# Holding the next weights' split behind the copies of the value blocks, and the output's last 512 columns as two products and two sums of 256

## The chip, the cores and the metric

One core of a Trainium2 chip runs the whole program in one launch. The metric is the time of one execution in microseconds, as the device reports it. The kernel before has three such runs and one more that was profiled.

## The reference

Two layers of an encoder trunk for 256 tokens of 1024 channels in float32. Cut to what matters here:

```
h = rms_norm(x, norm1_g[l])
aq, ak, av, bq, bk, bv, cq, ck, cv, dq, dk, dv, g = split_parts(h @ w_in[l])
o_a = diff_attention(rope(norm(aq)), rope(norm(ak)), av, ...)      # 4 heads
o_b = gqa_attention(axial_rope(norm(bq)), axial_rope(norm(bk)), bv)
o_c = dilated_attention(rope(norm(cq)), rope(norm(ck)), cv)        # 3 groups of 512 columns
o_d = neighbourhood_attention(norm(dq), norm(dk), dv, rpb[l])
merged = sum_i sigmoid(g_i) * (o_i @ w_branch[l, i])
x = x + merged @ w_out[l]
x = x + (silu(a) * b) @ w_down[l]      # a, b: convolved halves of rms_norm(x) @ w_up[l]
```

The columns of `w_in` that make `dv`, `av` and the three groups of `cv` are the "value blocks": five per layer.

## The kernel before, in words

Every weight matrix passes through as a row of jobs of 1 MB. A job's `load` (L277) is one transfer on SyncE's queue into one of three `w` buffers, issued three jobs ahead. A job's weights are cut into two halves, and `split` turns each half into a float32r pair: ScalarE casts it to `hi` (L288), VectorE subtracts to get `lo` (L292). There are five `hi` and five `lo` buffers. TensorE multiplies each half in three products per step, `hi` by the rounded activations, `lo` by them, and `hi` by the activations' rest (L345, L346, L347 in `mm3`). One half feeds twelve matmuls of 512 columns.

`run` walks through the jobs in order. For job j it issues the load, splits half 2j+3, calls what the table `sched` has for the place (j, -1), then four quarters of the job's matmuls with a second split behind the second quarter and the calls of `sched` behind each. The attention units, the copies and the transposes are all such calls. The accumulators of the weight products are four PSUM banks ("mm"), score and transpose tiles have three ("ts"), and one bank ("o") holds the attention's outputs and now and then a transpose. `ORDER` gives the sequence of blocks: qD kB kD qB kA vD qA vA gD0 kC1 kC0 qC1 ... vC0 ... vC1 vC2 and so on.

A value block (`vblock`) takes two jobs. Behind the last quarter of the second, `ev` copies its two accumulators into a `t4` buffer: for vD, vA and vC0 by two ScalarE copies of 512 columns (L838), for vC1 and vC2 by ScalarE and VectorE in halves (L844). For vD, sixteen small transfers on SyncE's queue then gather shifted windows of these values (`windows`, L854).

`behind` holds what is issued inside it to a place behind the named instructions. `self.hold` is a dictionary of such instructions by place, which `run` asks at two of its splits. The sequence of instructions on each engine is settled when the program is built, by a scheduler that lets a ready instruction pass one that is not ready. On the chip each engine then runs its list as written.

An attention unit of mixers A or B runs: two scores on TensorE (L545), maximum on VectorE (L626), two exponentials on ScalarE (L630), reciprocal on VectorE (L642), for B two scalings on ScalarE (L645), four transposes on TensorE (L549), a copy on ScalarE (L656), products with the values into "o" (L545), and a rounding of the result on ScalarE (L449) and VectorE (L455). For D the exponentials stand in L611.

At the end of the last layer `down` accumulates 256 x 1024 outputs in four banks, and `fin` adds each to the residual (L1194) and stores it by two transfers (L1197), one on SyncE's and one on ScalarE's queue.

Of the kernel before, what the change touches and what calls it, by code (L numbers as in the profile page):

```python
# [13 lines left out]
ALU = mybir.AluOpType  # L14
# [4 lines left out]
DEPTH = 2  # L19
# [70 lines left out]
class Trunk:  # L90
# [214 lines left out]
    def run(self):  # L305
        for j, job in enumerate(self.jobs):
            first, second = j in self.pairs, j - 1 in self.pairs
            self.load(j + LOAD_AHEAD)
            if not second and j > 1:
                self.split(2 * j + 3)  # L310
            for fn in self.sched.get((j, -1), []):
                fn()
            for q in range(4):

                src, sq = job, q
                if first:
                    src, sq = self.jobs[j + q // 2], q % 2
                elif second:
                    src, sq = self.jobs[j - 1 + q // 2], 2 + q % 2
                src["mm"](src["hl"], sq)  # L320
                if q == 1 and j not in self.late and j > 1:
                    with self.behind(self.hold.get((j, 0))):
                        self.split(2 * j + (3 if second else 4))
                for fn in self.sched.get((j, q), []):
                    fn()
            if second:
                with self.behind(self.hold.get((j, 1))):
                    self.split(2 * j + 4)
# [418 lines left out]
    def layer(self, l):  # L747
        nc = self.nc
        base = len(self.jobs)
        J = lambda s: base + s  # L750
# [30 lines left out]
        stt = [{"qT": {}, "kT": {}, "v": []} for _ in range(4)]  # L781
# [42 lines left out]
        def vblock(m, col0, g=0):  # L824
            cell = self.in_block(l, col0)
            slot[0] += 2
            e = slot[0] - 1

            def ev():
                v = stt[m]["v"]  # L830
                if g == 0:
                    v.append(self.t4([128, 2, 512]))
                elif g == 1:
                    v.extend([self.t4([128, 2, 512]), self.t4([128, 2, 512])])
                for t in range(2):
                    o = cell["o"][t]
                    if g == 0:
                        nc.scalar.copy(v[0][:, t, :], o)  # L838
                        continue

                    for b in range(2):
                        r = slice(64 * b, 64 * b + 64)
                        w = r if g == 1 else slice(64 - 64 * b, 128 - 64 * b)
                        (nc.scalar.copy if b == 0 else nc.vector.tensor_copy)(v[1 + t][w, b, :], o[r])  # L844

            def windows():

                v = stt[MD]["v"]
                for i in range(2):
                    v.append(self.t4([128, 2, 512]))  # L850
                for cb in range(4):
                    c0 = min(max(16 * cb - 8, 0), 32)
                    for u in range(4):
                        nc.sync.dma_start(v[1 + cb // 2][32 * u:32 * u + 32, cb % 2, :],  # L854
                                          v[0][64 * (u % 2) + c0:64 * (u % 2) + c0 + 32, u // 2, :])

            self.at(J(e), 3, ev)
            if m == MD:
                self.at(J(e + 1), 1, windows)
# [100 lines left out]
        for what in ORDER.split():  # L960
            kind, i, c = what[0], "ABCD".index(what[1]), int(what[2:] or 0)
            if what == "kB":
                bkv()
            elif kind in "qk":
                k = int(kind == "k")
# [198 lines left out]
        dacc = []  # L1164

        def down(i):
            def mm(hl, q):
                if not dacc:
                    dacc.extend([self.ps("ts"), self.ps("ts"), self.ps("ts"), self.ps("o")])
                steps = [(k, t) for k in range(2) for t in range(2)]  # L1170
                pairs = [(steps[q][0], steps[q][1], c) for c in range(2)]
                if i == 9:
                    pairs = [(q % 2, q // 2, c) for c in range(2)]
                if i == 10:
                    pairs = [(k, q // 2, q % 2) for k in range(2)]
                for k, t, c in pairs:
                    kt = 2 * i + k
                    g, gl = gh[kt // 4]
                    sl = slice(t * 128, (t + 1) * 128)
                    cs = slice(c * 512, (c + 1) * 512)  # L1180
                    self.mm3(dacc[2 * t + c][:, :], g[:, kt % 4, sl], gl[:, kt % 4, sl], hl[k][0][:, cs], hl[k][1][:, cs], kt == 0, kt == 21)

            self.add_jobs({"src": self.wsrc("w_down", l * DFF * DM, DM, i * 256, 2, 0, 1024), "mm": mm})
            slot[0] += 1
# [3 lines left out]
        e = slot[0] - 1  # L1188
        sst2 = {}

        def fin(t, c):
            cs = slice(c * 512, (c + 1) * 512)
            xs = self.x[:, t, cs]
            nc.vector.tensor_tensor(xs, xs, dacc[2 * t + c], ALU.add)  # L1194
            if l + 1 == DEPTH:
                for u in (2 * t, 2 * t + 1):
                    (nc.sync, nc.scalar)[u % 2].dma_start(self.rows("out", u, c * 512, 512), self.x[64 * (u % 2):64 * (u % 2) + 64, t, cs])  # L1197
                return
            if c == 0:
                sst2[t] = self.small("ss", 4)  # L1200
            self.sumsq(t, cs, sst2[t], c)
            if c == 1:
                xn = self.norm_vec(t, self.g1, sst2[t], 2)
                if t == 0:
                    self.hold[J(e), 0] = self.norm_tr(0, xn)
                else:
                    self.at(J(e + 1), 0, lambda: self.norm_tr(1, xn))
# [6 lines left out]
        for t in range(2):  # L1214
            for c in range(2):
                self.at(J(e - 1 + t), 2 + c, lambda t=t, c=c: fin(t, c))
# [129 lines left out]
```

## Time and profile before

| what | before |
|---|---|
| median of 3 runs | 1216.28 us (1216.18 to 1216.49) |
| the profiled execution's own time | 1213.31 us |
| its span | 1211.5 us |
| TensorE busy | 1195.5 us, 99% |
| VectorE busy | 907.7 us, 75% |
| ScalarE busy | 746.8 us, 62% |
| GpSimd busy | 180.1 us, 15% |
| moved by DMA | 212.01 MB, mean 175 GB/s |

The span is what the profile's records cover; the profiled execution's time also holds what lies around them, 1.8 us here. Busy shares are means over the whole span and say which engine leaves hardly any room: one at 99% is idle for 16 us in all, those of the beginning and the end among them.

### The profile page before, as it was taken

What the parts mean: (1) busy time and instruction counts of PE and PEld (TensorE: products, weight loads), DVE (VectorE), ACT (ScalarE), POOL (GpSimd) and SP (SyncE); (2) the same over time, 40 slices, a digit from 0 to 9 for tenths busy, and PEclk for the clock granted to TensorE, in tenths of its full rate; (3) what the DMA queues carried; (4) which work ended last, traced back from release to release, by engine and by line L of the source; (5) the groups of instructions that cost most, each with busy time, mean ns of one, the idle gap of its engine ahead of it and who ended that gap; (6) DMA issues with size and microseconds to landing.
All of it is one profiled execution on the core that took longest, in us unless ns stands there. A gap on an engine that the chain in (4) does not pass through costs nothing.

```text
span 1211.5 us, 17591 instructions
## 1 busy us (share of the span) xinstructions
PE 1195.5 (99%) x6656; PEld 992.9 (82%) x6656; DVE 907.7 (75%) x1491; ACT 746.8 (62%) x1311; POOL 180.1 (15%) x132
## 2 busy tenths in 40 slices
PE   8999999999999999999999999999999999999998
PEld 6887878887888888888878877788888888888886
DVE  6998777986565699988478868688855557889863
ACT  4557756556655476776355677655666545777751
POOL 0332130220000002121023211212200000121200
PEclk9999999999999999999999999999999999999999
DMA  8758355454554465566544754464544553655551
GB/s 281 229 168 242 105 174 170 143 191 174 160 187 143 138 203 172 171 203 208 209 161 156 216 198 140 151 197 144 187 142 140 174 174 105 209 191 171 194 213 66
DMA packets 127651, 212.01 MB, mean 175 GB/s; under 512 B 9069, under 2 KB 56781, under 8 KB 127566
## 3 DMA queue, kind: packets, MB, share of 16 engines
q1 hardware_dynamic: 125964, 206.16, 50.9%
q0 software_dynamic: 1280, 4.20, 1.6%
q8 instruction: 52, 0.85, 0.3%
q10 hardware_dynamic: 322, 0.53, 0.1%
q14 instruction: 33, 0.27, 0.1%
HBM read 203.53 MB, written 1.05 MB: 169 GB/s over the span
## 4 chain that ended last, share of the span: by engine, by line
PE 92%; DVE 4%; ACT 2%; issue 1%; POOL 0%; ACTq 0%; POOLq 0%; DVEq 0%
PE mm L345 18%; PE mm L346 18%; PE mm L347 18%; PE ts L1114 6%; PE mm L1114 5%; PE ts L545 4%; PE ts L1117 3%; PE mm L1117 3%; PE ts L347 2%; PE ts L346 2%; PE ts L345 2%; PE o L545 2%; PE ts L549 2%; DVE lo L292 2%; PE ts L515 1%; PE o L347 1%
## 5 line engine op out<-in xcount | busy, mean ns | idle before, releaser
L292 DVE TENSOR_TENSOR lo<-w,hi 128x1024 fp32r<-128x1024 f32 x376 | 457.4, 1225 | 176.2 <-ACT hi L288 172.6
L288 ACT CAST hi<-w 128x1024 fp32r<-128x1024 f32 x376 | 392.1, 1051 | 210.0 <-PE mm L347 155.9
L345 PE MATMUL mm<-hi,hT 128*128 128x512 f32 (+1 forms) x796 | 310.5, 392 | 2.4 <-DVE t L844 1.0
L346 PE MATMUL mm<-lo,hT 128*128 128x512 f32 (+1 forms) x796 | 308.2, 387 | 0.4 <-DVE lo L292 0.4
L347 PE MATMUL mm<-hi,hT 128*128 128x512 f32 (+1 forms) x796 | 307.5, 388 | 0.0
L345 PEld LDWEIGHTS mm<-hi,hT 128*128 128x128 f32 x796 | 149.7, 188 | 35.6 <-issue 2.9
L346 PEld LDWEIGHTS mm<-lo,hT 128*128 128x128 f32 x796 | 149.7, 188 | 30.3 <-issue 1.7
L347 PEld LDWEIGHTS mm<-hi,hT 128*128 128x128 f32 x796 | 149.5, 188 | 30.2 <-DVE hT L455 0.9
L1114 PE MATMUL mm<-hT,hi 128*128 128x512 f32 x352 | 124.4, 395 | 0.0
L1114 PE MATMUL ts<-hT,hi 128*128 128x512 f32 x320 | 114.2, 397 | 1.5 <-DVE e L1133 1.5
L1117 PE MATMUL mm<-hT,lo 128*128 128x256 f32 x352 | 94.7, 280 | 0.0
L1148 POOL TENSOR_TENSOR pt<-pt,e 128x256 f32<-128x256 f32 x44 | 58.1, 1339 | 223.3 <-DVE e L1144 203.4
L1117 PE MATMUL ts<-hT,lo 128*128 128x256 f32 x320 | 86.2, 280 | 0.0
L1114 PEld LDWEIGHTS mm<-hT,hi 128*128 128x128 f32 x352 | 65.8, 188 | 13.8 <-issue 0.2
L164 POOL TENSOR_TENSOR sm_qr<-sm_qr,mhalf 128x16 f32<-128x16 f32 (+1 forms) x24 | 74.7, 3111 | 2.0
L345 PE MATMUL mm<-hi,t 128*128 128x512 f32 (+1 forms) x192 | 73.5, 384 | 0.0
L346 PE MATMUL mm<-lo,t 128*128 128x512 f32 (+1 forms) x192 | 73.4, 382 | 0.0
L347 PE MATMUL mm<-hi,t 128*128 128x512 f32 (+1 forms) x192 | 72.9, 380 | 0.0
L1114 PEld LDWEIGHTS ts<-hT,hi 128*128 128x128 f32 x320 | 59.9, 188 | 15.5 <-DVE e L1133 3.1
L1117 PEld LDWEIGHTS mm<-hT,lo 128*128 128x128 f32 x352 | 66.2, 188 | 2.1 <-issue 0.2
L163 POOL TENSOR_SCALAR sm_qr<-sm_qr 128x16 f32<-128x16 f32 (+1 forms) x24 | 24.6, 1026 | 271.7 <-DVE sm_qr L504 271.6
L1117 PEld LDWEIGHTS ts<-hT,lo 128*128 128x128 f32 x320 | 60.1, 188 | 2.0 <-issue 0.2
(175 smaller groups left out, 1773.2 us busy)
## 6 DMA issues: line engine op xcount, KB each, us to landing
w<-in_w_in_dram SPq DMA_DIRECT2D x97, 1024.0 KB, 5.0
w<-in_w_up_dram SPq DMA_DIRECT2D x44, 1024.0 KB, 4.9
w<-in_w_down_dram SPq DMA_DIRECT2D x22, 1024.0 KB, 4.9
w<-in_w_branch_dram SPq DMA_DIRECT2D x16, 1024.0 KB, 5.0
w<-in_w_out_dram SPq DMA_DIRECT2D x8, 1024.0 KB, 4.9
t<-t POOLq DMA_DIRECT2D x16, 256.0 KB, 6.4
t<-t SPq DMA_DIRECT2D x32, 64.0 KB, 2.6
t<-in_rpb_dram SPq DMA_DIRECT2D x32, 62.5 KB, 5.5
```

What stands on the lines that cost most here:

```text
L163: nc.gpsimd.tensor_scalar(dst, ss, EPS, None, op0=ALU.add)
L164: nc.gpsimd.tensor_tensor(dst, dst, mh, ALU.pow)
L288: self.nc.scalar.copy(hi, w)
L292: self.last_split = self.nc.vector.tensor_tensor(lo, w, hi[:].bitcast(F32), ALU.subtract).ins
L345: mm(out, xh, wh, start=first, stop=False)
L346: mm(out, xh, wl, start=False, stop=False)
L347: self.last_mm = mm(out, xl, wh, start=False, stop=last).ins
L545: self.chain = (self.nc.tensor.matmul(out, stationary, moving, **kw).ins,)
L549: self.chain = (self.nc.tensor.transpose(out, src, self.ident).ins,)
L1114: wide = lambda: mm(o.rearrange("p (a s) -> p a s", a=2), h, self.hT[:, :, k, :], start=k == 0, stop=k == 7)
L1117: mm(o[:, :256], lo, self.hTh[:, k, :], start=False, stop=False)
L1148: nc.gpsimd.tensor_tensor(s[:, 256:], s[:, :256], y[:, 256:], ALU.mult)
```

## The change

Three edits. `ev` puts the last two of a value block's copies into `self.hold` for the job behind the block. `run` now asks this at the first split of each job, so that this split (its cast on ScalarE and its subtraction on VectorE) is issued behind these copies. And in the last layer the last quarter of the last job makes its 512 columns as two groups of 256, and `fin` adds and stores the last 512 columns in two steps of 256.

```diff
@@ run
             if not second and j > 1:
-                self.split(2 * j + 3)
+                with self.behind(self.hold.get((j, -1))):
+                    self.split(2 * j + 3)
@@ vblock, ev
-                v = stt[m]["v"]
+                v, copies = stt[m]["v"], []
...
                     if g == 0:
-                        nc.scalar.copy(v[0][:, t, :], o)
+                        copies = [nc.scalar.copy(v[0][:, t, :], o).ins]
                         continue
...
-                        (nc.scalar.copy if b == 0 else nc.vector.tensor_copy)(v[1 + t][w, b, :], o[r])
+                        copies.append((nc.scalar.copy if b == 0 else nc.vector.tensor_copy)(v[1 + t][w, b, :], o[r]).ins)
+
+                self.hold[J(e + 1), -1] = copies[-2:]
@@ down
+                if l + 1 == DEPTH and i == 10 and q == 3:
+
+                    pairs = [(k, 1, c) for c in (2, 3) for k in range(2)]
...
-                    cs = slice(c * 512, (c + 1) * 512)
-                    self.mm3(dacc[2 * t + c][:, :], g[:, kt % 4, sl], gl[:, kt % 4, sl], hl[k][0][:, cs], hl[k][1][:, cs], kt == 0, kt == 21)
+                    cs, out = slice(c * 512, (c + 1) * 512), dacc[2 * t + min(c, 1)]
+                    if len(pairs) == 4:
+                        cs, out = slice(c * 256, (c + 1) * 256), out[:, (c - 2) * 256:(c - 1) * 256]
+                    self.mm3(out, g[:, kt % 4, sl], gl[:, kt % 4, sl], hl[k][0][:, cs], hl[k][1][:, cs], kt == 0, kt == 21 and not (len(pairs) == 4 and c == 2))
@@ fin
+            if l + 1 == DEPTH:
+                n = 256 if (t, c) == (1, 1) else 512
+                for o in range(0, 512, n):
+                    cs = slice(c * 512 + o, c * 512 + o + n)
+                    xs = self.x[:, t, cs]
+                    nc.vector.tensor_tensor(xs, xs, dacc[2 * t + c][:, o:o + n], ALU.add)
+                    for u in (2 * t, 2 * t + 1):
+                        (nc.sync, nc.scalar)[u % 2].dma_start(self.rows("out", u, cs.start, n), self.x[64 * (u % 2):64 * (u % 2) + 64, t, cs])
+                return
             nc.vector.tensor_tensor(xs, xs, dacc[2 * t + c], ALU.add)
-            if l + 1 == DEPTH:
-                for u in (2 * t, 2 * t + 1):
-                    (nc.sync, nc.scalar)[u % 2].dma_start(self.rows("out", u, c * 512, 512), self.x[64 * (u % 2):64 * (u % 2) + 64, t, cs])
-                return
```

Line numbers behind the first edit are one higher in the change (L345 becomes L346, L838 becomes L839, L854 becomes L857). Because the scheduler builds a new sequence around the held splits, instructions move on every engine, nearly all of them around the value blocks; the number of each kind stays, but for the end's. Three places follow, all of the first layer; the second layer has the same three.

ScalarE around vA: `mm_1139` and `mm_1140` are vA's accumulators, `t_242_1310` the buffer they are copied to, `hi_1315` the half that the edit holds, `o_1281` an output of mixer D and `e_1218` the softmax of a unit of B. Before, two pieces of the list:

```order
L288 CAST hi_1237<-w_1133 128x1024 [waits DMAHW6_49,PE_49]
L288 CAST hi_1315<-w_1133 128x1024 [waits PE_49]
L656 COPY pt_1005<-ts_1004 128x512 [waits PE_49]
...
L656 COPY pt_1275<-ts_1274 128x512 [waits PE_49]
L449 CAST t_240_1298<-o_1281 128x16x16 x2
L838 COPY t_242_1310<-mm_1139 128x512
L838 COPY t_242_1310<-mm_1140 128x512
L288 CAST hi_1635<-w_1520 128x1024 [waits PE_49]
```

And in the change:

```order
L646 ACTIVATE e_1218<-e_1218,sm_cf_1227 128x256 [waits DVE_49]
L646 ACTIVATE e_1218<-e_1218,sm_cf_1227 128x256 [waits Activation_49]
L657 COPY pt_1268<-ts_1267 128x512 [waits PE_49]
L657 COPY pt_1275<-ts_1274 128x512 [waits PE_49]
L450 CAST t_240_1298<-o_1281 128x16x16 x2
L839 COPY t_242_1310<-mm_1139 128x512 [waits DMAHW7_49,DMAHW0_49]
L839 COPY t_242_1310<-mm_1140 128x512
L288 CAST hi_1315<-w_1133 128x1024
L288 CAST hi_1333<-w_1197 128x1024 [waits DMAHW7_49]
L288 CAST hi_1379<-w_1197 128x1024
```

The copies stand behind the same neighbours in both lists, those of `o_1281`; the cast of `hi_1315` and the casts that follow it (`hi_1333`, `hi_1379`, `hi_1395`, `hi_1458`, and five more that stood ahead of the copies before) have moved back behind them.

TensorE at the same place: `ts_1161` and `ts_1351` are scores of B, `ts_1209` the transposes of the softmax `e_1162` that comes out of `ts_1161`. Before:

```order
L346 MATMUL mm_1319<-lo_1316,hT 128x512
L545 MATMUL ts_1161<-t_78_466,t_126_725 128x256 [waits DVE_49,PE_49]
L545 MATMUL ts_1161<-t_78_466,t_126_725 128x256 x3
L347 MATMUL mm_1319<-hi_1315,hT 128x512
L345 MATMUL mm_1320<-hi_1315,hT 128x512
L346 MATMUL mm_1320<-lo_1316,hT 128x512
L347 MATMUL mm_1320<-hi_1315,hT 128x512
L345 MATMUL mm_1462<-hi_1333,hT 128x512 [waits Activation_49]
...
L549 MATMUL ts_1209<-ident,e_1162 128x128 [waits Activation_49]
```

And in the change, from the same scores to the first product with `hi_1315`:

```order
L348 MATMUL mm_1320<-hi_1237,hT 128x512
L546 MATMUL ts_1161<-t_78_466,t_126_725 128x256 [waits DVE_49,PE_49]
L546 MATMUL ts_1161<-t_78_466,t_126_725 128x256 x3
L550 MATMUL ts_1209<-ident,e_1162 128x128 [waits Activation_49]
...
L550 MATMUL ts_1267<-ident,e_1095 128x128 [waits DVE_49,Activation_49]
...
L550 MATMUL ts_1274<-ident,e_1094 128x128 [waits DVE_49,PE_49]
...
L550 MATMUL ts_1337<-ident,e_1218 128x128 [waits DVE_49,PE_49,Activation_49]
...
L546 MATMUL o_1344<-pt_1148,t_57_360 64x256 [waits DVE_49,PE_49]
...
L346 MATMUL mm_1319<-hi_1315,hT 128x512 [waits Activation_49]
```

Before, 38 weight products stood between `ts_1161` and `ts_1209`, and 58 more between `ts_1209` and `ts_1351`; in the change there is none from `ts_1161` to the product with `hi_1315`.

SyncE's queue around vD, whose windows are the rows of L854 (L857 in the change), and `w_1025` and `w_1133` the weights of gD0, the two jobs behind vA. One piece of the difference:

```order
 L277 DMA w_908<-in_w_in_dram 128x4x512
+L857 DMA t_177_974<-t_156_884 32x512 x8
+L857 DMA t_178_975<-t_156_884 32x512 x8
 L277 DMA w_1025<-in_w_in_dram 128x4x512
 L277 DMA w_1133<-in_w_in_dram 128x4x512
-L854 DMA t_177_974<-t_156_884 32x512 x8
-L854 DMA t_178_975<-t_156_884 32x512 x8
 L277 DMA w_1197<-in_w_in_dram 128x4x512
```

The two loads have moved behind the sixteen window transfers.

## Rows read from the trace of the kernel before

**Rows 1.** The page: busy time of TensorE, and the chain that ended last, by engine.
```profile
PE 1195.5 (99%) x6656; PEld 992.9 (82%) x6656; DVE 907.7 (75%) x1491; ACT 746.8 (62%) x1311; POOL 180.1 (15%) x132
...
PE 92%; DVE 4%; ACT 2%; issue 1%; POOL 0%; ACTq 0%; POOLq 0%; DVEq 0%
```

**Rows 2.** TensorE's waits by line and releaser: us in total, times, longest.
```profile
PE o L545 <- ACT pt L656: 1.6, 2, 0.8
...
PE mm L345 <- DVE t L844: 1.0, 2, 0.5
PE ts L545 <- ACT t L539: 0.9, 2, 0.5
```

**Rows 3.** Timeline of SyncE's queue at vD's windows, both layers: start us, us.
```profile
91.96 13.26 SPq L854 DMA_DIRECT2D t<-t  x16
...
689.94 12.55 SPq L854 DMA_DIRECT2D t<-t  x16
```

**Rows 4.** The page's DMA issues: KB each, us to landing.
```profile
w<-in_w_in_dram SPq DMA_DIRECT2D x97, 1024.0 KB, 5.0
```

**Rows 5.** Timeline of TensorE: first product with `hi_1181` (a half of `w_1025`), and its twin.
```profile
110.17 0.39 PE L345 MATMUL mm<-hi,hT 128*128 128x512 f32 x1
...
706.08 0.40 PE L345 MATMUL mm<-hi,hT 128*128 128x512 f32 x1
```

**Rows 6.** Timeline of ScalarE: casts of `hi_1237` and `hi_1315`, and vA's copies.
```profile
106.10 1.98 ACT L288 CAST hi<-w 128x1024 fp32r<-128x1024 f32 x2
...
144.16 1.12 ACT L838 COPY t<-mm 128x512 f32<-128x512 f32 x2
```

**Rows 7.** Timeline of TensorE: `ts_1161`, `ts_1209`, `o_1344`.
```profile
124.49 0.28 PE L545 MATMUL ts<-t,t 128*128 128x256 f32 x1
...
133.91 0.60 PE L549 MATMUL ts<-ident,e 128*128 128x128 f32 x4
...
151.66 1.08 PE L545 MATMUL o<-pt,t 128*64 128x256 f32 x8
```

**Rows 8.** Timeline of VectorE and ScalarE: one softmax of B, and the scores ahead.
```profile
152.67 0.74 PE L545 MATMUL ts<-t,t 128*128 128x256 f32 x4
...
153.45 0.69 DVE L626 TENSOR_REDUCE sm_mn<-ts 128x2 f32<-128x512 f32 x1 [0.28 <-PE ts L545]
...
127.52 0.48 ACT L630 ACTIVATE e<-ts,sm_mn 128x256 f32<-128x256 f32 x1
...
128.34 0.21 ACT L630 ACTIVATION_READ_ACCUMULATOR e<-ts,sm_mn 128x1 f32 x1
...
128.80 0.16 DVE L642 RECIPROCAL sm_cf<-sm_sums 128x2 f32<-128x2 f32 x1
...
129.00 0.91 ACT L645 ACTIVATE e<-e,sm_cf 128x256 f32<-128x256 f32 x2 [0.45 <-DVE sm_cf L642]
```

**Rows 9.** Timeline of ScalarE and VectorE: what empties `ts_1252`, `ts_1274`, `o_1281`.
```profile
140.53 1.18 ACT L449 CAST t<-ts 64x512 fp32r<-64x512 f32 x2
...
142.67 1.08 ACT L656 COPY pt<-ts 128x512 f32<-128x512 f32 x2
143.63 0.67 ACT L449 CAST t<-o 128x256 fp32r<-128x256 f32 x2
...
144.30 1.39 DVE L455 TENSOR_TENSOR t<-ts,t 64x512 fp32r<-64x512 f32 x2
...
146.98 0.76 DVE L455 TENSOR_TENSOR t<-o,t 128x256 fp32r<-128x256 f32 x2
```

**Rows 10.** Timeline at the end, and a sum of 256 columns by its line.
```profile
1207.13 0.69 DVE L1194 TENSOR_TENSOR x<-x,o 128x512 f32<-128x512 f32 x1 [0.67 <-PE o L347]
...
L1133 DVE TENSOR_TENSOR e<-e,mm x44: 405/412/421, 447.1 to 1154.0; 128x256 f32<-128x256 f32 x44
```

**Rows 11.** Windows at the start: us, busy of each engine, granted clock, DMA share, GB/s.
```profile
8.90:12.30 3.40, 3.40 (x12) 2.71 (x11) 0.43 (x2) 0.80 (x2) 0.00 (x0) 0.50 1.03 339
...
14.50:17.00 2.50, 1.33 (x6) 0.48 (x5) 1.83 (x4) 0.00 (x0) 0.55 (x1) 1.00 1.02 343
```

## The prediction

> **What bounds the kernel now.** I read the page first: TensorE is busy for 1195.5 us, 99% of the span, and the chain of work that ended last is TensorE for 92% [rows 1]. So nearly every microsecond that TensorE waits is a microsecond of the result, and an edit that leaves the work as it is can only pay through TensorE's waits. I then read those waits by line. Three of them stand at value blocks and come twice, once in each layer: 0.8 us at products that wait for a copy of transposes (beside vC0), 0.5 us where scores wait for a ScalarE copy and 0.5 us where a weight product waits for VectorE's copy of a bank (at vC1 and vC2) [rows 2]. That is all that the first two edits can take away directly: 1.6 + 1.0 + 0.9 = 3.5 us.
>
> The third view is the lists of each engine before and after, held against the timeline. For vA they show that ScalarE copied its two banks at 144.16 us, behind the roundings of `o_1281`, while the casts of `hi_1237` and of `hi_1315`, the held half, ran from 106.10 us on, 38 us earlier [rows 6]. In the change the copies keep their neighbours and it is the casts that move. So the edit makes the weights late there rather than the copies early.
>
> **vA, the main term.** Before, the scores `ts_1161` were at 124.49 us and the transposes of their softmax at 133.91 us [rows 7]; 38 weight products lay between, and the softmax cost TensorE nothing. In the change no weight product stands between `ts_1161` and the first with `hi_1315`, because the halves that would feed one are cast behind the copies. TensorE runs its list in order, so each step of the softmax is now bare. I walk it, with zero at the first score's start.
>
> First wait. The scores take 0.48 us of issue (four of 256 columns), the maximum starts 0.78 behind their start (153.45 against 152.67) and takes 0.69; two exponentials run from 127.52 to 128.55, 1.03; reciprocal 0.16, and the first half of the scalings about 0.5 of the pair's 0.91 [rows 8]. With some 0.2 for three handovers that is 0.78 + 0.69 + 1.03 + 0.16 + 0.5 + 0.2 = 3.4. TensorE was done at 0.5, and waits 2.9, and 0.2 more for the second half: 3.1 us.
>
> Second. The transposes `ts_1209` end near 4.3, the scores `ts_1217` near 4.8 and `ts_1243` near 5.2. `ts_1252` finds a bank and ends at 5.65. `ts_1267` needs the bank of `ts_1217`, which is free when its exponentials end: 5.8 + 1.03 = 6.9. Wait 1.25 us. `ts_1274` needs that of `ts_1243`, which two ScalarE roundings (1.18 for the pair) and two VectorE ones (1.39) empty [rows 9], from 6.9 on: first rounding 7.5, then VectorE's pair to 8.9. `ts_1267` ended at 7.35, so the wait is 1.55 us, and `ts_1274` ends at 9.35.
>
> Third. `o_1281` takes some 1.05 and ends at 10.4. Meanwhile ScalarE finishes the roundings of `ts_1252` (9.2), the scalings of `e_1218` (10.1), two copies of transposes (1.08: 11.2) and only then rounds `o_1281` (0.67: 11.9) [rows 9]. `ts_1337` starts about 10.5 and ends at 10.85. `o_1344` needs the single "o" bank, free when VectorE has taken its share of `o_1281`, the second half of the 0.76 behind 11.9 [rows 9]: 12.4. Wait 1.55 us. Its eight products take 1.0 and the scores 0.5, to 13.9. By then ScalarE has made vA's copies (1.12, to 13.0) and the cast of `hi_1315` (half of 1.98, to 14.0) [rows 6]; two products, and then `hi_1333` is ready near 15.0: waits of 0.15 and 0.5.
>
> The sum is 3.1 + 1.25 + 1.55 + 0.1 + 1.55 + 0.15 + 0.5 = 8.2 us for each layer. Behind it a cast of about 1 us feeds twelve products of 0.23, so no further wait follows. Bounds: 6, if the bank waits overlap better than I walked them, and 9.5, if VectorE's subtractions behind `hi_1315` are late as well.
>
> **SyncE's queue at vD.** The sixteen window transfers, which wait for vD's copies, took 13.26 us of the queue from 91.96 in layer 0 and 12.55 from 689.94 in layer 1 [rows 3]. Before, `w_1025` and `w_1133` were issued ahead of them; now they stand behind, so that `w_1025` is issued at 105.2 and 702.5, lands 5.0 us later [rows 4] and is cast 1 us after: 111.2 and 708.5. TensorE's first product with its half was at 110.17 and 706.08 [rows 5]. That is at most 1.1 and 2.4 us late. If vD's copies come a little earlier, now that no cast goes ahead of them, it is less; I take 0.6 and 1.5, with 0 and the full lateness as bounds. The casts held at vD itself have slack, since they are wanted a microsecond and more after the copies.
>
> **vC0, vC1 and vC2.** At vC0 six products now stand in front of the one that waited 0.8 us [rows 2], which hides it: -0.8 per layer, with +1 as the other bound should the cast behind the copies be late. At vC1 and vC2 the two waits of 0.5 go, but the cast of the next half now stands behind two copies; a pair of copies takes 1.1 us and the cast 1.0 [rows 6], of which I let 1.5 reach TensorE. Net +0.5 per layer, between -1.0 and +1.5.
>
> **The end.** The last sum is 0.69 us for 512 columns, and 0.41 is what the nearest sum of 256 took [rows 10], so the last store starts 0.28 us earlier and carries half the bytes. Twelve products replace six at the same number of columns; a longer issue of up to 0.1 us in all stands against it. Net -0.3, between -0.7 and +0.3.
>
> **The sum.** Layer 0: 8.2 + 0.6 - 0.8 + 0.5 = 8.5. Layer 1: 8.2 + 1.5 - 0.8 + 0.5 = 9.4. With the end: 17.6 us. The profiled execution took 1213.31 us, so one of the change should take about 1230.9; its median is 1216.28, 3.0 above, and I add the same to it: 1233.9 us. With all low bounds the sum is 2 x (6 - 0.8 - 1.0) - 0.7 = 7.7 (1224.0), with all high ones 2 x (9.5 + 1 + 1.5) + 3.5 + 0.3 = 27.8 (1244.1); both together are unlikely.
>
> **Rivals.** (1) Faster: the copies do what they say and the softmax stays covered, because the banks that come free let other products run beside it. Then only the waits of rows 2 go, 3.5 us, with the end's 0.3: 1212.5 us. For it speaks that vA held two of four banks until 144.16 us, 38 us behind the casts [rows 6]. The Trainium skill says in "PSUM — Partial Sum Buffer" (Summary: rules for kernel authors) that accumulators should be evacuated promptly because the memory is tight; by that rule the change is right. The trace agrees that the banks are held, yet its only waits for value copies are those of rows 2. Against it speaks the list: no product that could cover is left in front. It decides when vA's and the queue's terms together fall under 1.9 us per layer. Chance 6%.
>
> (2) Half: part of the walk is covered, say the bank waits (1.25 + 1.55 + 1.55 = 4.35 per layer) vanish, because ScalarE and VectorE keep up. The sum is then 17.6 - 8.7 = 8.9, and the time 1225.2. Against it: these waits come from durations that the trace shows. Chance 16%.
>
> (3) The clock: TensorE would idle in about five pieces of some 8 us out of 16 in each layer, and the granted clock could fall. At the start it was 0.50 (1.2 GHz) for 3.4 us while TensorE was busy without a break; in a stretch with 1.33 us of work in 2.50 it stayed at 1.00 (2.4 GHz) [rows 11]. One fall in each layer at the price of the start, half of 3.4 us or all of it, adds 3.4 to 6.8 us: 1237 to 1241. The only row like it kept the clock, so 10%. The Trainium skill, "TensorE: Matmul & The Clock Gate" (A second HAM failure mode: psum-queue depth-cycling), tells of short idle stretches between groups of products that lower the clock; no run here shows it yet.
>
> (4) No change: the scheduler's lists are those of the two programs, so the moves are certain; only gains and losses that cancel would give it. Chance 4%.
>
> **How the numbers follow.** My forecast, slower by 12 to 22 us, has 64%; its own range is 1228 to 1238. With the half (16%) and the clock (10%), slower holds 90%, same 4%, faster 6%. "Same" means within 0.2%, 2.4 us, about what a measurement of this kernel can tell from no change. A range of 1224 to 1241 takes in the forecast, most of the half and of the clock, and leaves less than 2 in 10 out.
>
> **What would show it.** Right: TensorE's waits at the transposes of `e_1162` (about 3 us), at two later transposes (1.2 to 1.6) and at the next "o" product (1.5), twice each; casts of weights directly behind vA's copies; TensorE's busy time unchanged and its share near 98%; the waits of rows 2 beside vC0 gone; a late first product with `w_1025`, more so in layer 1. Wrong: weight products seen between `ts_1161` and `ts_1209`, a clock under 1.00 around 130 us, or a time under 1224, which would mean that the walk double-counts waits that overlap.

## The result and the profile after

The change is slower: 1235.0 us median of 4 runs (1234.01 to 1240.55) against 1216.23 (1213.48 to 1216.49), a ratio of 1.0175 with an interval of 1.0156 to 1.0193, or 19.0 to 23.5 us. The profiled execution took 1235.5 us with a span of 1233.7, 22.2 us longer than before. Executions of one kernel can lie some 3 us apart (those of the kernel before at 1212.2 to 1213.4 and at 1215.9 to 1216.5 us), and traces part by as much within their first 20 us, so differences below 3 us are read here from ratios with intervals, or from places in a trace; the two profiled executions compared next start alike.

The page of the change, span and busy time (compare [rows 1]):

```profile
span 1233.7 us, 17612 instructions
...
PE 1205.4 (98%) x6662; PEld 1000.0 (81%) x6662; DVE 905.2 (73%) x1492; ACT 743.7 (60%) x1311; POOL 185.1 (15%) x132
```

TensorE has the same products to make (six more in number, because at the end twelve of half the width stand for six), but it is busy for 9.9 us longer, and it is idle for 1233.7 - 1205.4 = 28.3 us instead of 16.0. So the 22.2 us are 12.3 of waiting and 9.9 of slower work, net of what has gone. Its waits, by line and releaser: us in total, times, longest (compare [rows 2]):

```profile
PE ts L550 <- ACT e L646: 6.9, 2, 4.3
PE ts L550 <- DVE t L456: 3.3, 2, 1.8
PE o L546 <- DVE t L456: 3.1, 2, 1.5
...
PE mm L346 <- ACT hi L288: 1.7, 5, 0.5
PE mm L347 <- DVE lo L292: 1.5, 4, 0.4
```

The first three are new, come once in each layer and make 13.3 us. Those of [rows 2] are gone. The timeline of TensorE at vA in layer 0, the scores `ts_1161` first (compare [rows 7]):

```profile
123.58 0.63 PE L546 MATMUL ts<-t,t 128*128 128x256 f32 x4
126.86 0.84 PE L550 MATMUL ts<-ident,e 128*128 128x128 f32 x4 [2.65 <-ACT e L646]
...
130.01 1.12 PE L550 MATMUL ts<-ident,e 128*128 128x128 f32 x4 [0.32 <-ACT e L631]
132.58 1.09 PE L550 MATMUL ts<-ident,e 128*128 128x128 f32 x4 [1.45 <-DVE t L456]
133.60 1.98 PE L546 MATMUL o<-pt,t 128*64 128x64 f32 x32
...
138.17 1.98 PE L546 MATMUL o<-pt,t 128*64 128x256 f32 x8 [1.54 <-DVE t L456]
```

From the scores to the transposes of their softmax it is 3.3 us with nothing between, where before it was 9.4 us full of products. The same in layer 1, where the first wait is longer: ScalarE starts the exponentials at 732.95, behind the last of D's, though their maximum was done at 731.72, and VectorE makes the reciprocal at 734.53, behind D's products (L618), though the exponentials ended at 733.95.

```profile
735.28 1.00 PE L550 MATMUL ts<-ident,e 128*128 128x128 f32 x4 [4.29 <-ACT e L646]
...
741.54 0.63 PE L550 MATMUL ts<-ident,e 128*128 128x128 f32 x4 [1.81 <-DVE t L456]
...
746.25 1.98 PE L546 MATMUL o<-pt,t 128*64 128x256 f32 x8 [1.54 <-DVE t L456]
```

Windows of TensorE around these places (us, busy, granted clock, DMA share, GB/s):

```profile
123.00:127.00 4.00, 1.35 (x9) 1.00 0.00 0
128.00:141.50 13.50, 10.18 (x67) 0.51 0.00 1
735.50:750.00 14.50, 11.02 (x75) 0.65 0.03 6
```

Behind the first wait the clock stood at 0.51 of full speed, its lower level of 1.2 GHz for nearly all of 13.5 us, and at a mean of 0.65 in layer 1. The eight products `o_1344` took 1.98 us there and 1.08 before [rows 7]. An estimate from these two rows: 10.18 x 0.49 + 11.02 x 0.35 = 8.8 us of TensorE's 9.9 us of longer work are the lower clock. The DMA share of 0 in layer 0 fits loads that wait for `w` buffers, which the held casts keep.

ScalarE made vA's copies and then all the held casts in one row:

```profile
137.09 1.12 ACT L839 COPY t<-mm 128x512 f32<-128x512 f32 x2
138.04 4.88 ACT L288 CAST hi<-w 128x1024 fp32r<-128x1024 f32 x5
```

SyncE's queue at vD (compare [rows 3]), and TensorE's first product with `hi_1181`:

```profile
91.95 12.03 SPq L857 DMA_DIRECT2D t<-t  x16
104.51 8.89 SPq L277 DMA_DIRECT2D w<-in_w_in_dram  x4
```
```profile
110.67 0.73 PE L346 MATMUL mm<-hi,hT 128*128 128x512 f32 x2 [0.30 <-ACT hi L288]
```

The end, VectorE's last sums (compare [rows 10]): both begin only behind the last product, and together take 0.75 us where the one took 0.69.

```profile
1229.20 0.75 DVE L1207 TENSOR_TENSOR x<-x,o 128x256 f32<-128x256 f32 x2 [0.74 <-PE o L348]
```

### The profile page after: what moved, and what is told of

Read it like the earlier page. It is cut to its first block, busy times and chain, and to the rows that moved or that the text cites. A ratio compares the mean times of both kernels' runs of the same rounds, so it can differ in the third digit from the quotient of the medians.

```text
span 1233.7 us, 17612 instructions
## 1 busy us (share of the span) xinstructions
PE 1205.4 (98%) x6662; PEld 1000.0 (81%) x6662; DVE 905.2 (73%) x1492; ACT 743.7 (60%) x1311; POOL 185.1 (15%) x132
## 4 chain that ended last, share of the span: by engine, by line
PE 89%; DVE 5%; ACT 3%; issue 1%; DMA 1%; SPq 1%; POOL 0%; DVEq 0%; ACTq 0%
PE mm L347 17%; PE mm L348 17%; PE mm L346 17%; PE ts L1117 6%; PE mm L1117 5%; PE ts L546 3%; PE ts L1120 3%; PE mm L1120 3%; PE ts L348 2%; PE ts L347 2%; PE ts L346 2%; PE o L546 2%; PE ts L550 2%; DVE lo L292 2%; PE ts L516 1%
## 5 line engine op out<-in xcount | busy, mean ns | idle before, releaser
L346 PE MATMUL mm<-hi,hT 128*128 128x512 f32 (+1 forms) x796 | 303.9, 392 | 2.3 <-ACT hi L288 1.7
L346 PEld LDWEIGHTS mm<-hi,hT 128*128 128x128 f32 x796 | 149.3, 189 | 35.0 <-ACT hi L288 4.7
L164 POOL TENSOR_TENSOR sm_qr<-sm_qr,mhalf 128x16 f32<-128x16 f32 (+1 forms) x24 | 77.2, 3215 | 2.0
L346 PE MATMUL mm<-hi,t 128*128 128x512 f32 (+1 forms) x192 | 73.1, 384 | 0.0
L163 POOL TENSOR_SCALAR sm_qr<-sm_qr 128x16 f32<-128x16 f32 (+1 forms) x24 | 27.3, 1140 | 301.4 <-DVE sm_qr L505 301.4
```

Source lines behind the costliest of these rows:

```text
L163: nc.gpsimd.tensor_scalar(dst, ss, EPS, None, op0=ALU.add)
L164: nc.gpsimd.tensor_tensor(dst, dst, mh, ALU.pow)
L346: mm(out, xh, wh, start=first, stop=False)
```

## The experiments

They are to tell apart: the hold at vA through bare waits (theory T), the window transfers ahead of the loads (rival Q), the end (rival E); later, whether the clock is a part of its own (C against N), and whether a hold costs by itself (H) or because the copies that it waits for are late (L).

**1. The five holds alone.** `fin` and `down` as before, the rest as in the change.

> The five holds alone, the end as before. Theory T (the loss is vA's bare softmax, in waits and in a clock that falls with them): as the whole change, 18 to 22 us above before, 1234 to 1238. Rival E (the two-step end adds or takes something that counts): differs from the whole change by more than 1 us.

1235.31 us, ratio 1.0170 (1.0148 to 1.0191). That is the whole change's within the intervals, which are wider than rival E's 1 us. The loss is in the holds; run 2 bounds the end.

**2. The end alone.**

```diff
-                with self.behind(self.hold.get((j, -1))):
+                with self.behind(None):
```

> The end in two steps alone, no hold. T: within 0.5 us of before, because both sums of 256 in the trace of the change started only behind the last product (0.75 us for the two against 0.69 for one before). The prediction's own term was -0.3 us. Rival E: 1 us or more to either side.

Ratio 0.9996 (0.9984 to 1.0008), or 1.9 us faster to 1.0 us slower. Neither the prediction's -0.3 nor a gain of E's size can be told from nothing by that; the trace above says why there is no gain, since the first sum doesn't start earlier.

**3. The hold at vA alone** (on the kernel of 1, and so in 4, 8, 9 and 10 with other conditions).

```diff
-                self.hold[J(e + 1), -1] = copies[-2:]
+                if m == MA:
+                    self.hold[J(e + 1), -1] = copies[-2:]
```

> The hold at vA alone, in both layers. T: 19 to 22 us above before, no weight product between the scores and the transposes of B's fourth softmax, clock at 0.50 for some 7 to 13 us behind it, and TensorE busy for 9 to 10 us more than before with the same work. Rival Q (the window transfers ahead of two loads at vD make a good part): only 8 to 15 us above before.

1230.63 us, ratio 1.0138 (1.0118 to 1.0159), 14 to 19 us. That lies between what T and Q had said. The three waits are all there, one of each in each layer (7.1, 3.8 and 3.6 us for both layers); TensorE's busy time rose by 4.5 us rather than 9 to 10, because the clock recovered between two falls. Windows of TensorE, as above:

```profile
120.00:131.00 11.00, 6.15 (x40) 1.00 0.00 0
131.00:135.00 4.00, 3.14 (x38) 0.57 0.00 0
135.00:138.00 3.00, 0.99 (x10) 1.00 0.01 3
138.00:141.50 3.50, 3.50 (x15) 0.51 0.19 35
```

So the three waits come close to those of the whole change (14.5 us against 13.3), and how long the clock stays down behind them differs. It differs between executions of one kernel too: the four of run 1 took from 1231.8 us, at a mean granted clock of 0.995, to 1238.0, at 0.992. And here the first wait in layer 0, 2.84 us up to 126.14, left the clock at 1.00; it fell only at 131, behind the second and within the third.

**4. All holds but vA's** (`if m != MA`).

> The holds at vD, vC0, vC1 and vC2, not at vA. T: 0 to 2.5 us under before (1213.7 to 1216.2), clock 1.00 throughout, the waits beside vC0 gone. Rival Q: 4 us or more above before, with late first products of the loads that were moved behind the window transfers.

1226.28 us, ratio 1.0100 (1.0082 to 1.0118). T's number was a miss, and so was its clock of 1.00 throughout (0.54 from 218 to 225 us). Q's number was right, but not for Q's reason. The waits are not at the late loads: those on a softmax end at 218.68, 818.32 and 824.81 us, and the longest on `hi` at 279.99, by vC1 and vC2. TensorE's waits in this run:

```profile
PE ts L550 <- DVE e L641: 7.0, 3, 3.0
PE mm L347 <- DVE lo L292: 2.1, 4, 0.7
...
PE mm L346 <- ACT hi L288: 1.3, 3, 0.9
```

L641 is the last step of mixer A's softmax, and the timeline has the transposes that wait for it just ahead of vC0's copies, at 220.44 in layer 0. Where vA isn't held, vC0's hold does to A's units what vA's hold does to B's.

**5. Filling the first wait.** The hold at vA alone, with 20 products of 256 columns behind the scores of B's fourth unit. Their result goes to a score bank and is read by nothing.

```diff
-                self.chain = (self.last_mm,)
-                out = None
+                self.chain = (self.last_mm, *self.filled)
+                self.filled, out = (), None
...
+                if m == MB and i == 3:
+                    p = self.ps("ts")
+                    for r in range(20):
+                        self.mma(p[:, :256], self.hTh[:, 0, :128], self.hTh[:, 0, :], start=True, stop=True)
+                    self.filled = self.chain
```

> The hold at vA alone, and 20 extra products of 256 columns in each layer (2.4 us), of activations with themselves into a score bank that nothing reads, between the scores ts_1161 and the transposes that wait for their softmax. Theory C (the clock falls because of the bare waits): the waits stay, the extra products lie in the first of them, the granted clock stays at 1.00 longer, and the time is 1 to 5 us below the hold at vA alone (1230.6). Rival N (the clock has nothing to do with that wait): within 1 us of it. Rival P (the place was not empty): 2 to 5 us above it.

1226.53 us, ratio 1.0100 (1.0067 to 1.0134), 4.1 us less than 3 by the medians though it does more. The extra products lie in the wait. In layer 0 it has 0.44 us left and the clock never fell; in layer 1 1.90 us is left and the clock did fall, for some 3.5 us. Timeline and windows of TensorE:

```profile
122.21 2.56 PE L547 MATMUL ts<-hT 128*128 128x256 f32 x20
125.21 0.84 PE L551 MATMUL ts<-ident,e 128*128 128x128 f32 x4 [0.44 <-ACT e L647]
```
```profile
120.00:142.00 22.00, 17.73 (x132) 1.00 0.21 69
730.00:736.00 6.00, 3.12 (x48) 1.00 0.01 3
736.00:740.00 4.00, 4.00 (x18) 0.57 0.21 45
```

The intervals of 3 and 5 overlap a little, and the four times of 5 are far apart (1223.0, 1224.1, 1229.0 and 1230.6 us), so it is the trace, of the first of these, that carries this: the later waits are still there (1.87, 0.40 and 1.56 us), most of the first is filled, and the clock is at 1.00 instead of two stretches at 0.5 in layer 0. TensorE is busy for 1199.5 us in it, against 1200.0 in 3, though some 5 us of products came on top. That profile is 6.1 us shorter than the one of 3, of which 0.9 lie before 20 us. This speaks for C and against N: the clock's fall is a cost of its own and has to do with the idle time. That this one wait sets it off is not shown.

**6 and 7. vA's copies with a buffer of their own**, with the hold at vA (6) and without any (7).

```diff
-        return self.sb(self.ap, "t4", shape, dt, bufs=18)
+        return self.sb(self.ap, "t4", shape, dt, bufs=17)
...
-                if g == 0:
+                if m == MA:
+                    v.append(self.sb(self.ap, "va", [128, 2, 512], F32, bufs=1))
+                elif g == 0:
```

> The hold at vA alone, but vA's copies go to a buffer of their own (t4 has 17 instead of 18, so the memory is the same). Theory L (the hold costs because the copies come late, and they come late because no t4 buffer is free until mixer D's unit is done): the copies run near 111 us, weight products stand between the scores and the transposes as before, and the time is within 2 us of the next kernel's, near 1213 to 1218. Rival H (a hold at this split costs by itself): 8 to 15 us above the next kernel.

> The kernel before with vA's own buffer and 17 in t4, no hold: the control of the last one. L and H: 1212 to 1218, as the copies of vA were no bound in the kernel before.

Ratios to the kernel before: 1.0009 (0.9998 to 1.0020) with the hold, 1.0002 (0.9986 to 1.0018) without. The hold that cost 14 to 19 us costs nothing that shows. TensorE in 6 has no idle time around vA (window, busy, clock, DMA share, GB/s), nor from 700 to 760 us in layer 1:

```profile
110.00:145.00 35.00, 35.00 (x229) 1.00 0.52 182
```

ScalarE in 6, copies at 109.7 and 111.1 us, as soon as TensorE has ended each accumulator, and the held casts right behind:

```profile
106.14 1.04 ACT L288 CAST hi<-w 128x1024 fp32r<-128x1024 f32 x1
109.71 0.59 ACT L841 COPY va<-mm 128x512 f32<-128x512 f32 x1 [1.51 <-PE mm L348]
111.11 0.59 ACT L841 COPY va<-mm 128x512 f32<-128x512 f32 x1
111.57 2.02 ACT L288 CAST hi<-w 128x1024 fp32r<-128x1024 f32 x2
```

That is L, at vA: the hold costs what the copies are late, and vA's copies are late because no `t4` buffer is free. What keeps those buffers was not tested.

**8. The hold at vC0 alone** (`if m == MC and g == 0`).

> The hold at vC0 alone. Theory L, from the run of all holds but vA's, whose TensorE waited 3.0 us for a softmax of mixer A ahead of vC0's copies in each layer, with the clock down behind it: 8 to 12 us above before. The prediction's own term (a wait of 0.8 us per layer goes and nothing comes): 1.6 us below before. Rival Q (the window transfers at vD made the loss of that run): within 2 us of before.

1220.85 us, ratio 1.0046 (1.0028 to 1.0065), 3.4 to 7.9 us. Less than I expected from 4, but the other way than the prediction's term of -1.6. TensorE waits 3.0 us for A's softmax in both layers, and the clock falls:

```profile
221.92 0.74 PE L550 MATMUL ts<-ident,e 128*128 128x128 f32 x4 [3.03 <-DVE e L641]
```
```profile
222.00:232.00 10.00, 10.00 (x47) 0.83 0.42 144
```

**9. The hold at vD alone** (`if m == MD`).

> The hold at vD alone, which puts the sixteen window transfers ahead of two loads on SyncE's queue. The prediction's terms: 0.6 us in layer 0 and 1.5 in layer 1, together 2.1 above before. Theory S (what the trace of the change shows, waits of 0.3 and 0.2 us there): 0.2 to 1.5 us above before. Rival Q (a late load is paid in full): 3.5 us above.

Ratio 1.0016 (1.0003 to 1.0029), 0.4 to 3.5 us: the prediction's 2.1 fits in, and so does S; Q is at the edge. The trace has waits of 0.55 us at `hi_1181` in layer 0 and 0.27 at a `lo` near its twin in layer 1 (708.32), which is S's size.

**10. The hold at vC1 and vC2 alone** (`if g > 0`).

> The hold at vC1 and vC2 alone. The prediction's terms: 0.5 us in each layer, together 1.0 above before. Theory L (copies at vC1 and vC2 are not late, so the hold moves little): within 2 us of before. Rival D (what the run of all holds but vA's lost beyond the hold at vC0 alone comes from here): 4 to 6 us above.

1219.81 us, ratio 1.0042 (1.0025 to 1.0058), 3.0 to 7.1 us. A miss for L and for the prediction's 1.0; rival D's 4 to 6 us lies inside. So a late copy is not the only way in which a hold costs. The held casts come behind the copies in one row, and TensorE waits for the first of them; then the clock falls. In layer 1 the same waits (0.89, 0.22 and 0.68 us) left the clock at 1.00. TensorE and ScalarE in layer 0:

```profile
279.00 0.73 PE L346 MATMUL mm<-hi,hT 128*128 128x512 f32 x2 [0.89 <-ACT hi L288]
...
280.00:284.00 4.00, 3.60 (x9) 0.57 0.31 96
```
```profile
276.94 1.06 ACT L845 COPY t<-mm 64x512 f32<-64x512 f32 x2
277.89 3.89 ACT L288 CAST hi<-w 128x1024 fp32r<-128x1024 f32 x4
```

In this profile some 3 of its 6.5 us lie before 20 us, where the kernels don't differ. The remaining 3.5 are, by estimate, these waits in both layers (3.3 us) less those of [rows 2] that they replace (1.9), and about 1.6 us of half clock (3.60 x 0.43).

**11 and 12. Two buffers of their own, for vA and vC0**, in the whole change (11) and in the kernel before (12).

```diff
-        return self.sb(self.ap, "t4", shape, dt, bufs=18)
+        return self.sb(self.ap, "t4", shape, dt, bufs=16)
...
-                if g == 0:
+                if g == 0 and m != MD:
+                    v.append(self.sb(self.ap, "va", [128, 2, 512], F32, bufs=2))
+                elif g == 0:
```

> The whole change, with two buffers of their own for the copies of vA and vC0 (t4 has 16 instead of 18). Theory L: the 19 us are gone, 1212 to 1218; TensorE's waits for softmaxes near vA and vC0 and the stretches at half clock are absent. Rival H (holds cost by themselves): 1225 or more.

> The kernel before with the same two buffers and 16 in t4: the control of the last one. Theory L: 1211 to 1217, within 2 us of the last one. Rival M (two fewer t4 buffers hurt elsewhere): 3 us or more above before.

Ratios 1.0077 (1.0059 to 1.0094) and 1.0047 (1.0029 to 1.0064), medians of 1223.93 and 1220.68 us: both outside what L gave. M is right: with 16 buffers left, something else is late, and without any hold TensorE waits twice for 2.5 us on a normalisation. In 12:

```profile
PE mm L345 <- DVE qn L502: 5.0, 2, 2.5
```

Beside that control the whole change costs 0.30%, 3.7 us, instead of 21; each ratio has an interval of some 2 us to either side. The waits on a softmax are absent from 11's waits, and the clock is at 1.00 from 110 to 145 us and from 705 to 760, but the stretches of lower clock are not all gone as L had said: they stand behind a wait for the normalisation (0.72 from 264 to 270 us) and at vC1 and vC2; 11's waits on `hi` (2.6 us) and `lo` (1.8 us) are like those of 9 and 10, whose holds it still has.

## Why the prediction was right

The time, 1233.9 forecast and 1235.0 measured, came out by the mechanism that the sum rests on. That it came so close is in part luck: the sum had 17.6 us of waits at an unchanged clock, the trace has 12.3 us of waits and 9.9 of slower work. The loss by the ratio is 19.0 to 23.5 us, so 17.6 was too small, and the two medians, 18.8 apart, hide some of that. Two of the prediction's signs of being right failed (TensorE's busy time unchanged; the late load showing more in layer 1), and one of its signs of being wrong appeared: a clock under 1.00 around 130 us.

*vA's hold makes the weights late.* Right, and shown from three sides: alone it costs 14 to 19 us (3), without it the five holds cost 9 us less (4 against 1), and with copies that come early it costs nothing (6 and 7). The place, the order of the waits and what each waits for are those of the walk.

*The walk's size.* 8.2 us per layer forecast. Layer 0 had 2.65 + 0.32 + 1.45 + 1.54 = 5.96, layer 1 had 4.29 + 1.81 + 1.54 = 7.64 with its short one below those listed. The wait for the bank of `ts_1217` was forecast at 1.25 and was 0.32; eight transposes ahead of it already ran at half clock (1.68 us), which took up part of it. The first was forecast at 3.1 and was 2.65 and 4.29: the walk left out that ScalarE and VectorE still had D's softmax to finish in layer 1.

*The clock.* I gave it 10% as a rival. It happened, in both layers, and is some 8.8 us, by the estimate above, of the 22.2 us of the profiled execution, where the rival had priced it at 3.4 to 6.8; run 5 speaks for its hanging on the idle time. The step that failed is leaving it out of the sum because "the only row like it kept the clock" [rows 11]: one row with 1.17 us idle in 2.50 said too little about 6 us idle in the 18 us from 123.58. The Trainium skill, "TensorE: Matmul & The Clock Gate" (A second HAM failure mode: psum-queue depth-cycling), tells of a kernel whose frequent short idle stretches between groups of products made the clock swing between its two levels. The trace of run 3 agrees, with 0.57, 1.00 and 0.51 in turn from 131 to 141.5 us. That the result stayed in the range is because the waits were oversized by 17.6 - 12.3 = 5.3 us and the clock, which the sum left out, came to more than that.

*SyncE's queue.* Forecast 0.6 and 1.5; alone it is 0.4 to 3.5 for both (9). In the change 0.30 us of it shows at `hi_1181`, and in layer 1, where more was forecast, 0.18 at a `lo` there: the second size is wrong, and why the lateness did not show is open. `w_1025` was issued at 104.5, against 105.2 in the walk.

*vC0.* Forecast -0.8 per layer. In the change the wait is gone, as said. But the term was read from the combination: alone the hold costs 3.4 to 7.9 us (8). The single holds add up to about 29 us by their ratios' middles and the whole costs 21, and in the whole change, whose lists there are others, the waits of 3.0 us that vC0's hold brings alone are absent.

*vC1 and vC2.* Forecast +0.5 per layer, measured 3.0 to 7.1 for both (10): mis-sized, again with the clock in it. In the whole change the trace has waits of 0.48, 0.22 and 0.44 us there in layer 0 (285.75 to 287.88), nearly the same in layer 1, in place of 0.47 and 0.49, at a clock of 1.00: net +0.2 per layer, so there the forecast was a little high.

*The end.* Forecast -0.3. The two sums both waited for the last product (1229.20), so the step that takes one sum of 256 (0.41 us) as the part behind the last product failed: both were there, 0.75 us together. Its time is within 1.9 us of nothing (2).

## What to carry to other kernels

Before you hold work behind an instruction, ask when that instruction can run, not when its input is ready: vA's sums were complete near 111 us and with a buffer of their own were copied there (6), but in the change the copies ran only at 137, and the hold handed this lateness to every weight behind it. Where TensorE is at 99%, covering work is what hides the small chains; taking it away cost the chain here, and then clock as well. An effect of one hold in a schedule that is built anew is not what it is alone: compare lists, and test each against a control.

## What the runs showed that I had not expected

The clock fell to its lower level behind waits of quite different kinds: one of 2.65 us (at 128 us in the change), two of 0.89 and 0.22 us that came close together (it was down from 280.5 us in run 10, before the third, of 0.40, had ended), and one of 3.03 us (run 8, at 0.83 in the mean of ten microseconds). Behind waits of 0.8 and 0.5 us in the kernel before it stayed at 1.00. And the same waits did not always do the same: those of run 10 left it at 1.00 in layer 1, one of 2.51 us in run 11 was followed by 0.72 in layer 0 (264 to 270 us) and its twin by 1.00 in layer 1 (866 to 872). So the length of a wait alone does not decide. What exactly does is open.
